# Queries and keys of the dilated groups stay in natural order, and TensorE reads every fourth column of them

## The chip, the cores and the metric

The kernel runs on one core of a Trainium2 chip. The metric is the time of one execution on the device in microseconds, the median of the runs shown. One more execution was taken by the profiler; the views below are of that one. Engines are named as in the profile: PE is TensorE's matmuls, PEld its loads of the stationary operand, DVE is VectorE, ACT is ScalarE, POOL is GpSimd and SP is SyncE.

## The reference, cut to what matters

Two layers over 512 positions of width 1024, in float32. Each layer is a half feed-forward step, a mixer, a second half feed-forward step and a gated embedding. The mixer of layer 0 (the even one) holds two attentions that share one projection: a windowed one, and a dilated one, which the change touches. The dilated one has 12 heads of 64, in three groups of four slots, and the outputs of the three groups are merged by their softmax denominators:

```python
B_PAIRS = ((128, 1), (512, 4), (2048, 16))        # window, dilation of the three groups
def dilated_attention(q, k, v):
    for gi, (window, dil) in enumerate(B_PAIRS):
        def to_res(t):        # positions sorted into residue classes modulo dil
            return t.reshape(bsz, sub, dil, B_SLOTS, dh).transpose(0, 2, 1, 3, 4).reshape(bsz * dil, sub, B_SLOTS, dh)
        o, lse = banded_attention(to_res(q), to_res(k), to_res(v), window // (2 * dil))
```

`q` and `k` have a rotary embedding before that: each half of a head's 64 features is multiplied by a cosine of the position and gets the other half times a sine added.

## The kernel before, in words

Activations lie with features on the 128 partitions and the 512 positions along the free dimension, 4 bytes each. Weights are split into a high and a low part, and each product of the projections is three matmuls of 128x128 by 128x512 (`mm3`, lines 171 to 173).

The even mixer (`ab`, line 621) is a list of attention steps (`a_steps`, `b_steps`) into which a second list, the projections and value projections (`fill`), is woven by weights written out by hand (`weave`, line 714): a projection is put in front of the step that needs it, or earlier where its share of the work has come. TensorE works through its part of this in program order, so while VectorE and ScalarE prepare a step's operands, TensorE runs a projection.

The dilated attention handles two slots at a time (`sp` is 0 or 1). For each slot pair, `proj_b` projects and rotates the queries and keys of group 0 (`stacked`) and of groups 1 and 2 (`proj`); the latter stay in plain float32. `rope` (line 578) is where a projection leaves PSUM: two VectorE instructions multiply it by the sine (L595, into `u`) and by the cosine (L596, into `o`), each reading the 512 columns of the PSUM bank in order, and four DMAs with an accumulating write (L599, issued from GpSimd's queue) add the 32-row pieces of `u` to the swapped pieces of `o`. `kind` gives the order in which the two instructions write: "n" natural, "b" (queries of group 0) by blocks of 128 and, within them, by residue modulo 4, and "r" (groups 1 and 2) by residue modulo 4 over all 512 positions, so that a write in kind "r" hops 128 elements from one column to the next. Twenty ropes run in the mixer: ten "n", two "b", eight "r".

In `b_steps`, `soft` makes the scores. Group 0 goes through `scores` (L612, L613). For groups 1 and 2 there is, for each residue r, one product of 64x128 by 64x128 for each group (L820), with 128 contiguous columns of `bq` as the stationary and of `bk` as the moving operand, since kind "r" has sorted them; the profile shows each such float32 product as two matmul records. A VectorE reduction with the mask follows (L824), the exponentials are ScalarE's (L830). `merge` combines the denominators of the groups with small copies between partitions (L840, L857) and scales all exponentials (L861); `pv_r` transposes the scaled tiles on TensorE (L870), copies them out (L872) and multiplies them with the values (L876); `pv_n` does the same for group 0 (`windows_pv`: L531, L147 and L148, L541 and L542), and L891 adds the two, reading both of its sources in hops. L906 is an addition of the same size without hops.

Of the kernel before, what the change touches and what calls it, by code (L numbers as in the profile page):

```python
# [15 lines left out]
P = 128  # L16
# [29 lines left out]
class Trunk:  # L46
# [530 lines left out]

    def rope(self, p, kind):


        nc = self.nc
        if self.cosr is None:
            self.cosr, self.sinr = self.act(), self.act()
            nc.vector.tensor_tensor(self.cosr, self.rot[0], self.R, op=ALU.mult)
            nc.vector.tensor_tensor(self.sinr, self.rot[1], self.R, op=ALU.mult)

        o, u = self.act(), self.tmp()
        if kind == "n":
            v = w = lambda x: x
        elif kind == "r":  # L590
            v, w = (lambda x: x.rearrange("p (r a) -> p a r", r=4)), (lambda x: x.rearrange("p (a r) -> p a r", r=4))
        else:
            v, w = (lambda x: x.rearrange("p (b r a) -> p b a r", b=NB, r=4)), (lambda x: x.rearrange("p (b a r) -> p b a r", b=NB, r=4))
        with self.tc.high_priority():
            nc.vector.tensor_tensor(v(u), w(p), w(self.sinr), op=ALU.mult)  # L595
            nc.vector.tensor_tensor(v(o), w(p), w(self.cosr), op=ALU.mult)  # L596
        for i in range(4):
            j = i ^ 1
            nc.gpsimd.dma_start(o[i * 32:(i + 1) * 32, :], u[j * 32:(j + 1) * 32, :], accum_op=ALU.add)  # L599
        return o  # L600
# [20 lines left out]
    def ab(self, k_next):  # L621
        nc, io = self.nc, self.io
        cos, sin = self.act(), self.act()
        nc.sync.dma_start(cos, io["cos"])
        nc.sync.dma_start(sin, io["sin"])
        self.rot, self.cosr = (cos, sin), None
        m_a, m_b0, m_br = self.act(), self.act(), self.act()
        nc.sync.dma_start(m_a[:, :384], io["mask_a"])
        nc.sync.dma_start(m_b0[:, :384], io["mask_b0"])
        nc.sync.dma_start(m_br[:, :256], io["mask_br"])  # L630
        sink = self.small("sink", [P, 12])
        nc.sync.dma_start(sink, io["sink"].partition_broadcast(P))
        self.turn, self.alone = 1, True
        mix = [None] * KC
        w = io["qk_ab"]

        nat = lambda x, b: x[:, b * P:(b + 1) * P]
        v = {}

        t = {}  # L640

        def proj(key, i, kind):
            return [(key, 1, lambda: t.__setitem__(key, self.rope(self.project(w[i]), kind)))]

        def stacked(key, i, kind, p=None):

            c = []

            def stack():
                if key[0][1] == "k":  # L650
                    low = self.lows()
                    t[key] = (self.stack_k(c[0], low), low)
                else:
                    t[key] = self.stack_q(c[0])

            return [(key + (0,), 1, lambda: c.append(self.rope(p or self.project(w[i]), kind))), (key, 0, stack)]

        def behind_next(*items):

            out, rest = [], []  # L660
            for first, *second in items:
                out += [first] + rest
                rest = second
            return out + rest

        def proj_a(gp):
            return [stacked(("ak", gp), 12 + 4 * gp, "n")] + [
                stacked(("aq", gp, j), 13 + 4 * gp + j, "n") for j in range(3)]

        def proj_b(sp):  # L670
            out = [stacked(("bk", sp, 0), 6 * sp + 1, "n"), stacked(("bq", sp, 0), 6 * sp, "b")]
            for g in (1, 2):
                out.append(proj(("bq", sp, g), 6 * sp + 2 * g, "r"))
                out.append(proj(("bk", sp, g), 6 * sp + 2 * g + 1, "r"))
            return out

        def proj_v(key, i):
            if i < 2:
                f = lambda: v.__setitem__(key, self.project_v(io["v_ab"][i], nat, self.rcol))
            else:  # L680
                f = lambda: v.__setitem__(key, self.residues(
                    self.project_v(io["v_ab"][i], nat, self.rcol, parts=False)))
            return [(key, 2.4, f)]


        p = [self.project(w[12 + i], self.sbank()) for i in range(2)]
        with self.tc.issue_after(self.last_mm.ins):
            self.R
        fill = behind_next(stacked(("ak", 0), 12, "n", p[0]), stacked(("aq", 0, 0), 13, "n", p[1]), proj_v("va", 0),
                           *proj_a(0)[2:], *proj_a(1), *proj_b(0), proj_v("vb", 1), proj_v(("vr", 0), 2),  # L690
                           *proj_b(1), proj_v(("vr", 1), 3))
        steps = (self.a_steps(0, t, v, m_a, sink, mix) + self.a_steps(1, t, v, m_a, sink, mix)
                 + self.b_steps(0, t, v, m_b0, m_br, mix) + self.b_steps(1, t, v, m_b0, m_br, mix))
        fill += [(("o", m), PART, lambda m=m: self.out_part(io["o_ab"], m, mix, range(6))) for m in range(OPEN)]
        for _ in range(6):
            fill.pop(0)[2]()
        kept = self.put_away()

        first = steps[0][2]

        def behind():
            with self.tc.issue_after(self.last_mm.ins):
                first()

        steps[0] = steps[0][0], steps[0][1], behind

        for i in BEGIN_B:
            steps[i - 2] = steps[i - 2][0] + steps[i][0], *steps[i - 2][1:]
        self.weave(steps, fill, after={("o", 0): BEGIN_B[0]})
        self.alone = False  # L710
        self.out_proj(io["o_ab"], mix, 6, k_next, kept)
# [85 lines left out]
    def b_steps(self, sp, t, v, m_b0, m_br, mix):  # L797
# [4 lines left out]
        nc = self.nc  # L802
        c = {}

        def soft(hf):

            if hf == 0:
                c["st"] = self.small("st_b", [P, 2, 2, 2, 4])
            st = c["st"][:, hf]
            ng = self.small("ng_b", [P, 2, 4])  # L810
            e0 = [self.scores(t["bq", sp, 0], t["bk", sp, 0], hf, b, (m_b0, st[:, 0, 0, b:b + 1])) for b in range(NB)]
            rows = slice(hf * HD, (hf + 1) * HD)
            er = []
            for r in range(0, 4, 2):
                s = self.sbank()
                e = self.act()
                for i in range(2):
                    rr = slice((r + i) * P, (r + i + 1) * P)
                    for g in (1, 2):
                        nc.tensor.matmul(s[:, (2 * i + g - 1) * P:(2 * i + g) * P], t["bq", sp, g][rows, rr],  # L820
                                         t["bk", sp, g][rows, rr], start=True, stop=True)
                for i in range(2):
                    x = slice(2 * i * P, 2 * (i + 1) * P)
                    nc.vector.tensor_tensor_reduce(e[:, x], s[:, x], m_br[:, :256], op0=ALU.add, op1=ALU.max,  # L824
                                                   scale=0.125, scalar=-3e38, accum_out=st[:, 0, 1, r + i:r + i + 1])
                    er.append(e[:, x])
            nc.vector.tensor_scalar_mul(ng, st[:, 0], -1.0)
            for g, es in ((0, e0), (1, er)):
                for i, e in enumerate(es):
                    nc.scalar.activation(e, e, AF.Exp, bias=ng[:, g, i:i + 1], accum_out=st[:, 1, g, i:i + 1])  # L830
            c["e0", hf], c["er", hf] = e0, er
# [51 lines left out]
        def pv_n(hf):  # L883
# [9 lines left out]
            if hf:  # L893
                mix[6 + sp] = self.split_chunk(c["raw"], nc.vector)

        qk = [(x, sp, g) for x in ("bq", "bk") for g in range(3)]
        return [(qk, 1.5, lambda: soft(0)), (qk, 1.5, lambda: soft(1)), ([], 2, merge),
                ([("vr", sp)], .7, pv_r), (["vb"], 1.2, lambda: pv_n(0)), ([], 1.2, lambda: pv_n(1))]

# [384 lines left out]
```

## Time and profile before

| what | value |
|---|---|
| median of 3 runs | 2052.24 us (2050.88 to 2056.14) |
| the profiled execution, its own time | 2054.03 us |
| its span in the profile | 2052.3 us |
| mean granted clock of TensorE | 0.995 |
| busy: PE, PEld, DVE, ACT, POOL | 99%, 88%, 68%, 49%, 11% of the span |
| the even mixer | about 369 to 663 us of the span |

[...]

### The profile page before, as it was taken

What the parts mean: (1) busy time and instruction counts of PE and PEld (TensorE: products, weight loads), DVE (VectorE), ACT (ScalarE), POOL (GpSimd) and SP (SyncE); (2) the same over time, 40 slices, a digit from 0 to 9 for tenths busy, and PEclk for the clock granted to TensorE, in tenths of its full rate; (3) what the DMA queues carried; (4) which work ended last, traced back from release to release, by engine and by line L of the source; (5) the groups of instructions that cost most, each with busy time, mean ns of one, the idle gap of its engine ahead of it and who ended that gap; (6) DMA issues with size and microseconds to landing.
All of it is one profiled execution on the core that took longest, in us unless ns stands there. A gap on an engine that the chain in (4) does not pass through costs nothing.

```text
span 2052.3 us, 32118 instructions
## 1 busy us (share of the span) xinstructions
PE 2025.7 (99%) x12398; PEld 1806.6 (88%) x12398; DVE 1389.3 (68%) x2389; ACT 1008.5 (49%) x1702; POOL 229.0 (11%) x230
## 2 busy tenths in 40 slices
PE   9999999999999999999999999999999999999998
PEld 6999988888778899988888999888888889998886
DVE  8888733598866888843468888434778688885344
ACT  6555522476544555532345555323666545554232
POOL 0001011332212000001110000011000100000111
PEclk9999999999999999999999999999999999999999
DMA  6666543453335466643344665544333446764331
GB/s 196 181 184 181 162 131 129 113 114 82 85 75 176 107 182 181 167 148 111 118 134 125 183 180 158 154 132 141 107 103 112 154 107 168 188 178 134 111 108 42
DMA packets 111515, 284.25 MB, mean 139 GB/s; under 512 B 21761, under 2 KB 29441, under 8 KB 111361
## 3 DMA queue, kind: packets, MB, share of 16 engines
q1 hardware_dynamic: 97584, 241.26, 36.4%
q0 software_dynamic: 13632, 40.90, 12.7%
q8 instruction: 97, 1.59, 0.3%
q14 instruction: 58, 0.47, 0.1%
q10 hardware_dynamic: 144, 0.04, 0.0%
HBM read 258.03 MB, written 13.07 MB: 132 GB/s over the span
## 4 chain that ended last, share of the span: by engine, by line
PE 89%; DVE 4%; ACT 2%; issue 2%; DMA 1%; POOL 1%; SPq 0%; DVEq 0%; ACTq 0%; POOLq 0%
PE mm L172 10%; PE mm L171 10%; PE mm L173 10%; PE mm L360 6%; PE mm L359 6%; PE mm L358 6%; PE sc L171 6%; PE sc L173 6%; PE sc L172 6%; PE sc L360 3%; PE sc L358 3%; PE sc L359 3%; PE ob L358 2%; PE ob L360 2%; PE ob L359 2%
## 5 line engine op out<-in xcount | busy, mean ns | idle before, releaser
L147 ACT ACTIVATE wh<-wr 128x1024 fp32r<-128x1024 f32 (+2 forms) x431 | 446.5, 1038 | 641.2 <-PE mm L172 180.6
L148 DVE TENSOR_TENSOR wl<-wr,wh 128x1024 fp32r<-128x1024 f32 (+2 forms) x431 | 518.1, 1204 | 336.3 <-ACT wh L147 334.0
L171 PE MATMUL mm<-act,wh 128*128 128x512 f32 (+1 forms) x1000 | 391.8, 392 | 0.7 <-ACT act L197 0.4
L172 PE MATMUL mm<-act,wh 128*128 128x512 f32 (+1 forms) x1000 | 391.1, 391 | 0.7 <-DVE act L198 0.6
L173 PE MATMUL mm<-act,wl 128*128 128x512 f32 (+1 forms) x1000 | 390.2, 390 | 0.0
L360 PE MATMUL mm<-act,wl 128*128 128x256 f32 x1088 | 307.9, 283 | 0.0
L359 PE MATMUL mm<-act,wh 128*128 128x256 f32 x1088 | 307.9, 283 | 0.0
L358 PE MATMUL mm<-act,wh 128*128 128x256 f32 x1088 | 307.9, 283 | 0.0
L173 PE MATMUL sc<-act,wl 128*128 128x512 f32 x610 | 237.3, 389 | 0.4 <-DVE wl L148 0.4
L171 PE MATMUL sc<-act,wh 128*128 128x512 f32 x610 | 237.3, 389 | 0.0
L172 PE MATMUL sc<-act,wh 128*128 128x512 f32 x610 | 237.1, 389 | 0.0
L172 PEld LDWEIGHTS mm<-act,wh 128*128 128x128 f32 x1000 | 188.4, 188 | 38.3 <-DVE act L198 2.2
L171 PEld LDWEIGHTS mm<-act,wh 128*128 128x128 f32 x1000 | 188.3, 188 | 37.3 <-ACT act L197 0.9
L173 PEld LDWEIGHTS mm<-act,wl 128*128 128x128 f32 x1000 | 188.3, 188 | 36.0
L359 PEld LDWEIGHTS mm<-act,wh 128*128 128x128 f32 x1088 | 208.9, 192 | 0.4
L360 PEld LDWEIGHTS mm<-act,wl 128*128 128x128 f32 x1088 | 208.9, 192 | 0.2
L358 PEld LDWEIGHTS mm<-act,wh 128*128 128x128 f32 x1088 | 208.9, 192 | 0.2
L212 POOL TENSOR_TENSOR ssq<-ssq,tmp 128x512 f32<-128x512 f32 x48 | 76.3, 1590 | 864.0 <-ACT tmp L205 670.3
L358 PE MATMUL sc<-act,wh 128*128 128x256 f32 x544 | 154.0, 283 | 0.0
L359 PE MATMUL sc<-act,wh 128*128 128x256 f32 x544 | 154.0, 283 | 0.0
L360 PE MATMUL sc<-act,wl 128*128 128x256 f32 x544 | 154.0, 283 | 0.0
L173 PEld LDWEIGHTS sc<-act,wl 128*128 128x128 f32 x610 | 114.5, 188 | 24.1 <-DVE wl L148 0.6
(177 smaller groups left out, 3427.5 us busy)
## 6 DMA issues: line engine op xcount, KB each, us to landing
wr<-in_gu_dram SPq DMA_DIRECT2D x176, 512.0 KB, 4.6
wr<-in_gu_dram POOLq DMA_DIRECT2D x68, 512.0 KB, 5.5
wr<-in_dn_dram SPq DMA_DIRECT2D x64, 512.0 KB, 3.6
rb<-in_gu_dram SPq DMA_DIRECT2D x68, 256.0 KB, 3.0
wr<-in_dn_dram SPq DMA_DIRECT2D x32, 384.0 KB, 3.5
kept<-act SPq DMA_DIRECT2D x40, 256.0 KB, 2.2
wr<-in_qk_ab_dram SPq DMA_DIRECT2D x20, 512.0 KB, 3.3
act<-kept SPq DMA_DIRECT2D x40, 256.0 KB, 4.3
```

The source lines that it names most:

```text
L147: self.put(self.nc.scalar.activation(hi, src, AF.Copy))
L148: self.put((lo_eng or self.nc.vector).tensor_tensor(lo, src, hi.bitcast(F32), op=ALU.subtract))
L171: mm(out, stat[0], mov[0], start=start, stop=False)
L172: mm(out, stat[0], mov[1], start=False, stop=False)
L173: return mm(out, stat[1], mov[0], start=False, stop=stop)
L212: eng.tensor_tensor(self.acc, self.acc, sq, op=ALU.add)
L358: mm(out, w[0][:, c], xs[k][0][:, x], start=start and k == 0, stop=False, skip_group_check=True)
L359: mm(out, w[0][:, c], xs[k][1][:, x], start=False, stop=False, skip_group_check=True)
L360: mm(out, w[1][:, c], xs[k][0][:, x], start=False, stop=stop and k == half - 1, skip_group_check=True)
```

## The change

`rope` loses its kind "r", the projections of groups 1 and 2 use kind "n" instead, so that their queries and keys stay in natural order, and L820 takes the columns of a residue with a step of four, in the stationary and in the moving operand. Values, masks and everything behind the scores stay as they are, since the scores come out in the same order as before.

```diff
@@ def rope(self, p, kind):
         if kind == "n":
             v = w = lambda x: x
-        elif kind == "r":
-            v, w = (lambda x: x.rearrange("p (r a) -> p a r", r=4)), (lambda x: x.rearrange("p (a r) -> p a r", r=4))
         else:
@@ def proj_b(sp):
             for g in (1, 2):
-                out.append(proj(("bq", sp, g), 6 * sp + 2 * g, "r"))
-                out.append(proj(("bk", sp, g), 6 * sp + 2 * g + 1, "r"))
+                out.append(proj(("bq", sp, g), 6 * sp + 2 * g, "n"))
+                out.append(proj(("bk", sp, g), 6 * sp + 2 * g + 1, "n"))
             return out
@@ def soft(hf):
                 for i in range(2):
-                    rr = slice((r + i) * P, (r + i + 1) * P)
                     for g in (1, 2):
-                        nc.tensor.matmul(s[:, (2 * i + g - 1) * P:(2 * i + g) * P], t["bq", sp, g][rows, rr],
-                                         t["bk", sp, g][rows, rr], start=True, stop=True)
+                        nc.tensor.matmul(s[:, (2 * i + g - 1) * P:(2 * i + g) * P], t["bq", sp, g][rows, r + i::4],
+                                         t["bk", sp, g][rows, r + i::4], start=True, stop=True)
```

## Rows read from the trace of the kernel before

**Rows 1.** Head of the page: busy time (share of span) xinstructions.

```profile
span 2052.3 us, 32118 instructions
PE 2025.7 (99%) x12398; PEld 1806.6 (88%) x12398; DVE 1389.3 (68%) x2389; ACT 1008.5 (49%) x1702; POOL 229.0 (11%) x230
```

**Rows 2.** The chain that ended last, shares of the span by engine.

```profile
PE 89%; DVE 4%; ACT 2%; issue 2%; DMA 1%; POOL 1%; SPq 0%; DVEq 0%; ACTq 0%; POOLq 0%
```

**Rows 3.** Stretches: length, busy us (xinstructions) of PE, PEld, DVE, ACT, POOL, clock, DMA.

```profile
440.00:487.00 47.00, 46.21 (x241) 37.02 (x240) 43.11 (x99) 31.07 (x72) 18.12 (x24) 1.00 0.53 105
487.00:512.00 25.00, 24.80 (x194) 23.96 (x193) 19.92 (x61) 18.09 (x49) 3.19 (x4) 1.00 0.30 76
...
545.00:553.50 8.50, 8.50 (x39) 6.95 (x37) 8.14 (x26) 5.92 (x12) 3.44 (x7) 1.00 0.54 127
553.50:557.60 4.10, 0.29 (x2) 0.00 (x0) 3.81 (x21) 0.00 (x0) 1.48 (x2) 0.78 0.89 181
557.60:562.60 5.00, 4.96 (x15) 4.00 (x16) 5.00 (x16) 0.00 (x0) 0.00 (x0) 0.50 0.01 1
562.60:576.00 13.40, 13.32 (x91) 10.39 (x91) 7.75 (x11) 5.86 (x11) 3.18 (x4) 1.00 0.42 99
576.00:580.00 4.00, 3.18 (x24) 2.60 (x21) 4.00 (x6) 1.83 (x3) 2.31 (x5) 1.00 0.22 23
...
603.00:607.40 4.40, 2.53 (x12) 1.75 (x11) 3.81 (x24) 1.11 (x3) 0.00 (x0) 1.00 0.17 54
```

**Rows 4.** Waits of TensorE, 440 to 630 us: total, times, longest.

```profile
PE tr L870 <- DVE act L861: 5.7, 2, 3.9
PE ob L542 <- DVE tmp L148: 0.7, 1, 0.7
PE sc L612 <- DVE st_b L613: 0.5, 1, 0.5
```

**Rows 5.** Timeline of DVE: start, duration, engine, line, operation.

```profile
528.50 0.69 DVE L595 TENSOR_TENSOR tmp<-mm,act 128x512 f32<-128x512 f32 x1 [0.96 <-PE mm L173]
529.11 0.68 DVE L596 TENSOR_TENSOR act<-mm,act 128x512 f32<-128x512 f32 x1
...
547.23 1.11 DVE L595 TENSOR_TENSOR tmp<-mm,act 128x512 f32<-128x512 f32 x1
548.16 1.39 DVE L465 TENSOR_TENSOR act<-act,act 64x512 fp32r<-64x512 f32 x2
...
550.17 1.09 DVE L596 TENSOR_TENSOR act<-mm,act 128x512 f32<-128x512 f32 x1
...
576.08 1.09 DVE L596 TENSOR_TENSOR act<-mm,act 128x512 f32<-128x512 f32 x1
577.01 1.08 DVE L595 TENSOR_TENSOR tmp<-mm,act 128x512 f32<-128x512 f32 x1
577.92 1.06 DVE L596 TENSOR_TENSOR act<-mm,act 128x512 f32<-128x512 f32 x1
578.83 0.41 DVE L148 TENSOR_TENSOR tmp<-tr,tmp 128x256 fp32r<-128x256 f32 x1
```

**Rows 6.** Timeline of PE, same columns; x16 are sixteen records merged.

```profile
532.57 2.05 PE L820 MATMUL sc<-act,act 64*128 64x128 f32 x16
534.54 0.50 PE L172 MATMUL mm<-act,wh 128*128 128x512 f32 x1
...
557.64 0.69 PE L870 MATMUL tr<-ident,act 128*128 128x128 f32 x2 [3.85 <-DVE act L861]
...
563.35 1.15 PE L876 MATMUL ob<-tmp,act 128*64 128x128 f32 x16
...
579.29 0.39 PE L542 MATMUL ob<-tmp,act 128*128 128x256 f32 x1 [0.75 <-DVE tmp L148]
```

**Rows 7.** Groups of instructions by form: busy us, mean ns of one.

```profile
L891 DVE TENSOR_TENSOR act<-tmp,tmp 64x512 f32<-64x512 f32 x4 | 4.9, 1235 | 0.1
L906 DVE TENSOR_TENSOR tmp<-ob,tmp 64x512 f32<-64x512 f32 x4 | 2.7, 683 | 5.0 <-ACT tmp L905 5.0
```

## The prediction

> **What bounds the kernel now.** I read the head of the profile first: the matmul row of TensorE is busy for 2025.7 of 2052.3 us, so all of its idle time is 26.6 us, and every other engine has slack [rows 1]. The chain of work that ended last says the same: 89% of it is TensorE, 4% VectorE [rows 2]. What VectorE saves therefore shows in the time only where TensorE stands and waits for VectorE, and what TensorE loses shows nearly everywhere. The table by stretches looks for such places in the even mixer, from 440 us, where the first rope of a dilated group is still to come, to the last merge at 607 us [rows 3]. [...] The waits name the releasers: the two merges (L870 after the scaling at L861) 5.7 us in two waits, the longest 3.9; L542 after the low part of a transposed tile at L148, 0.7; L612 after a score reduction, 0.5 [rows 4]. These are the only doors through which a faster VectorE can shorten the run.
>
> **Part 1: the rope's two VectorE writes.** The change lets eight of the twenty ropes (two slot pairs, groups 1 and 2, q and k) write in natural order. Each is two instructions, L595 and L596, so 16 instructions change their write from one that hops 128 elements between neighbours to a plain one. Both kinds are in the trace, with the same reads from PSUM and SBUF [rows 5]. A plain one (528.50) lasts 0.69 us and the next starts 0.61 us behind it. A hopping one (547.23, 550.17, 576.08, 577.01, 577.92) lasts 1.06 to 1.11 and the next instruction starts 0.91 to 0.93 behind it (547.23, 576.08, 577.01, 577.92). The start to start difference is what VectorE gains: 0.31 us each, 16 x 0.31 = 5.0 us of VectorE's time. That is the whole possible gain, and most of it lies under TensorE's work. Door by door:
>
> The merge of slot pair 0. VectorE is at work nearly without a pause on the way to the scaling that TensorE waits for (8.14 of the 8.5 us from 545 to 553.5, and on through the gap [rows 3]), and two hopping writes of one rope stand in its queue, at 547.23 and 550.17. With both plain, the small copies and the scaling behind them come 0.6 us sooner, and TensorE's wait of 3.85 us, which ends at 557.64 [rows 6], becomes about 3.2. Gain 0.6 us. Bounds: if the chain is held by ScalarE's exponentials rather than VectorE, 0; if the shorter gap leaves the clock up, the 5.0 us at 0.50 become 2.5, so 0.6 + 2.5 = 3.1 us.
>
> The wait of L542 at 579.29 for the L148 at 578.83. In front of that L148 stand three hopping writes in a row (576.08, 577.01, 577.92), of which the last two belong to one rope and delay it, with the first, by 0.9 us. TensorE waited 0.75 us there [rows 6]; this door closes. Gain 0.75 us, bounds 0 (something else just as late, for instance ScalarE's part of the same tile) and 0.82, all the idle time of that stretch.
>
> The fourth rope of slot pair 1 writes between 562.8 and 564.8, in a stretch in which TensorE is idle for 0.08 us in all [rows 3]: worth nothing. The eight writes of slot pair 0 stand between 460 and 487 us. TensorE's whole idle time there and up to 512 is 0.79 + 0.20 = 0.99 us, in pieces, and only part of it waits for VectorE (the 0.5 us of L612). I take 0.2 us, bounds 0 and 0.99.
>
> The second merge, at 607.36, has no rope in front of it any more (the last ends at 578.8), so its 1.87 us stay. The two ropes of group 0 kept in their own order and the ten plain ones are untouched. The accumulating DMAs at L599, four for each rope, move the same rows of 512 contiguous elements, in the same number, from the same queue, and no wait is added: a rope's copies may start a little sooner, no more. The sum of part 1 is -0.6 - 0.75 - 0.2 = -1.55 us.
>
> **Part 2: TensorE reads every fourth column.** L820 issues 32 products, seen as 64 matmul records of 64x128 with one load of 128 columns each. Both operands now step four elements (16 bytes) between columns, the stationary and the moving one. Sixteen of them run from 532.57 to 534.54, 0.123 us each. No row of the trace shows TensorE reading with such a step, so I bound it. Below by 0: a stepped read has no reason to be quicker than a plain one. How near the memory these streams run can be read from L876: the same 128 moving columns against only 64 loaded ones take 1.15 / 16 = 0.072 us [rows 6]. So the moving stream has at least 0.05 us to spare for each record, and the load has none: 64 columns more cost 0.05 us, 0.8 ns a column, and any slowing of the load shows in full. Above by what a hop costs VectorE: the hopping write 0.31 us / 512 = 0.61 ns an element; or the two-source hopping read of L891 against the plain L906, 1.235 - 0.683 = 0.55 us / 512 = 1.08 ns [rows 7]. On 64 x 128 = 8192 loaded columns that is 5.0 us or 8.8 us, all on TensorE, which is busy in these stretches. I take 0: both prices are those of another engine's ports with other instructions, and the rows nearest to it, L820 and L876 on TensorE itself [rows 6], say that its load takes 0.8 ns a column where its moving stream needs at most 0.072 us / 128 = 0.56 ns for one, so that the load is not at the pace that these ports can read. This is the weakest step, and both ends stay in the range.
>
> [...]
>
> **Sum.** -1.55 + 0 = -1.55 us. The profiled execution took 2054.03 us (span 2052.3 and 1.7 around it), so it would take 2052.5. It lies 1.8 us above the median of the runs shown, 2052.24; from that median the same sum gives 2050.7 us.
>
> **The rivals.**
> *TensorE pays for the step.* This is the one that ends on the other side. Place: the 64 loads of L820. Price 5.0 to 8.8 us, net of part 1 +3.5 to +7.3, that is 2055.7 to 2059.5 us. It decides the sign as soon as a record takes 1.55 / 64 = 0.024 us more than 0.123; it is told from no change (0.3%, 6.2 us, about what a measurement of this kernel can tell) when it takes 7.7 / 64 = 0.12 us more, twice today's pace. For it: the load has no slack, and VectorE's rows show that this memory makes hopping streams dearer by half or more. Against it: the ports are others, and the moving side has slack.
> *Nothing reaches the end.* VectorE's 5 us all lie under TensorE, or what is gained at 557 and 579 is lost at the next wait (the second merge waits for ScalarE's exponentials and the 16 copies at L857 whatever came earlier). Then 2052.2 us. For it: 99% busy. Against it: the two waits whose releasers stand right behind hopping writes.
> [...]
> *Another order.* The program orders instructions of several queues around the ropes (L595 and its L596 are often split by others, as at 547.23 and 550.17). If the shorter operations lead to another order, waits of the size seen in rows 4 may open or close: 2 to 7 us either way.
>
> **How the numbers follow.** Forecast 46%, nothing reaches the end 12%, the clock stays up 8%, TensorE pays 26% (half of it, 13%, above +6.2, since both reads of a record may pay, one after the other), another order 8% (of which 4% faster by more than 6.2, 2% slower by more). Faster by over 0.3% needs 6.2 us, more than all of part 1's bounds add up to (3.1 + 0.82 + 0.99 = 4.9), so it is left to another order and what was overlooked: 6%. Slower by over 0.3%: 13 + 2 + 1 for what was overlooked = 16%. Within: 78% (the two shares for what was overlooked come off the forecast). The forecast's own range is 2048.5 to 2052.5; the range that should hold 8 in 10 reaches down to all of part 1's gains, 2052.2 - 4.9 = 2047.3, and up to the dearer price short of its end, 2059.
>
> **What the changed profile would show.** L595 and L596: sixteen fewer at 1.06 to 1.1 us, leaving two hopping ropes; the VectorE total falls by some 5 us. The wait of L870 at the first merge near 3.2 us and no wait of L542 for L148 show the doors right; the same waits unchanged show rival two. The sixteen records of L820: 1.97 us from the first to the next matmul if the step is free; 3.2 us or more if it pays. The granted clock behind the first merge: 0.50 for some 5 us, or not at all. The forecast is wrong if L820 takes over 2.4 us for sixteen, or if a new wait of more than 1 us appears on TensorE.

## The result, and the profile after

The changed kernel takes 2063.47 us in the median of 6 runs (2058.91 to 2067.34), the kernel before 2054.76 us on the same chip (6 runs, 2050.88 to 2056.19). The ratio is 1.0046 with a 95% interval of 1.0036 to 1.0055, that is +9.4 us (7.4 to 11.3): slower, and above the range that was forecast. (The ratio is the one estimated from the single runs, here and below, and not exactly that of the two medians.) The profiled execution of the changed kernel took 2058.91 us, the quickest of its six: its mean granted clock (the profile gives TensorE's clock as a share of full speed) is 0.996, that of the slowest run 0.991, so the trace shows less of what the clock costs than the median does.

Each engine's instructions stand in the same order in both programs; sixteen of VectorE's have another access pattern, and so have TensorE's score products. So every difference between the traces is one of durations and of what follows from them. Lines have moved up by three or four: L592 and L593 are L595 and L596 of before, L609 is L612, L816 is L820, L857 is L861, L866 is L870.

The head of the page after, and the chain by engine, as in [rows 1, 2]:

```profile
span 2057.1 us, 32118 instructions
PE 2031.2 (99%) x12398; PEld 1813.6 (88%) x12398; DVE 1384.3 (67%) x2389; ACT 1007.3 (49%) x1702; POOL 228.9 (11%) x230
...
PE 90%; DVE 3%; ACT 2%; issue 2%; DMA 1%; POOL 1%; SPq 0%; DVEq 0%; ACTq 0%; POOLq 0%
```

VectorE's busy time fell by 5.0 us, just as forecast, TensorE's rose by 5.5. The timeline of VectorE after shows the writes that stood in front of the low part L148 in [rows 5]:

```profile
577.63 0.68 DVE L593 TENSOR_TENSOR act<-mm,act 128x512 f32<-128x512 f32 x1
578.23 0.68 DVE L592 TENSOR_TENSOR tmp<-mm,act 128x512 f32<-128x512 f32 x1
578.83 0.68 DVE L593 TENSOR_TENSOR act<-mm,act 128x512 f32<-128x512 f32 x1
579.42 0.41 DVE L148 TENSOR_TENSOR tmp<-tr,tmp 128x256 fp32r<-128x256 f32 x1
```

The writes last 0.68 us in place of 1.06 to 1.09, and the next starts 0.60 us behind. The waits of TensorE after, for [rows 4]:

```profile
PE tr L866 <- DVE act L857: 5.1, 2, 3.2
PE sc L609 <- DVE st_b L610: 0.5, 1, 0.5
PE sc L609 <- DVE st_a L610: 0.3, 1, 0.3
```

The wait at the first merge went from 3.9 to 3.2 us, and that of L542 for L148 is gone. So VectorE's part came as forecast at these two doors. What it was traded for stands in the timeline of TensorE after, for [rows 6]:

```profile
529.70 0.39 PE L173 MATMUL mm<-act,wl 128*128 128x512 f32 x1
529.93 0.40 PE L171 MATMUL mm<-act,wh 128*128 128x512 f32 x1
530.26 4.13 PE L816 MATMUL sc<-act,act 64*128 64x128 f32 x16
534.32 0.79 PE L172 MATMUL mm<-act,wh 128*128 128x512 f32 x1
534.91 0.63 PE L609 MATMUL sc<-act,act 128*128 128x256 f32 x2
535.34 0.63 PE L173 MATMUL mm<-act,wl 128*128 128x512 f32 x1
```

From the first of the sixteen records to the next matmul it is now 534.32 - 530.26 = 4.06 us, 0.254 us a record, where it was 1.97 us and 0.123. (Records overlap in the rows: the L173 at 529.70 lasts 0.39 us, and the next begins 0.23 us behind it, so pace is read from start to start. Both averages hold some 0.2 us for the two ends of a block; within it a record starts every 0.235 us, where it was 0.112, as the rows under e7 show.) And the matmuls behind the block last 0.63 us, where those ahead of it last 0.39. The table by stretches says why, and answers to [rows 3]:

```profile
512.00:545.00 33.00, 33.00 (x168) 28.69 (x167) 19.27 (x56) 16.93 (x44) 4.22 (x6) 0.95 0.27 73
...
556.70:560.10 3.40, 0.22 (x1) 0.00 (x0) 3.11 (x21) 0.00 (x0) 0.63 (x1) 1.00 0.86 201
560.10:564.80 4.70, 4.64 (x18) 3.57 (x18) 4.70 (x17) 0.30 (x1) 0.00 (x0) 0.64 0.01 1
...
578.00:582.00 4.00, 3.93 (x32) 3.64 (x31) 3.86 (x7) 2.21 (x4) 3.16 (x7) 1.00 0.40 40
...
533.90:537.50 3.60, 3.60 (x13) 2.99 (x12) 1.34 (x8) 1.37 (x5) 0.00 (x0) 0.54 0.39 134
```

From 512 to 545 us the profile shows no gap on TensorE, and yet the mean granted clock is 0.95: from 533.9 to 537.5, at the end of the first stepped block and behind it, the mean is 0.54, so that nearly all of this stretch is at 0.50 (all of 534.0 to 537.0 is). The gap in front of L866 ends before the clock falls now, but it falls behind it (0.64 from 560.1 to 564.8).

Both traces can be laid side by side at the same instructions, with the chain's rows. First the kernel before:

```profile
371.57 1.12 PE tr L238 x4
...
414.62 0.58 PE sc L612 x4
...
532.63 1.98 PE sc L820 x16
537.72 1.98 PE sc L820 x16
...
588.94 1.98 PE sc L820 x16
594.06 1.98 PE sc L820 x16
...
661.28 0.79 PE tr L219 x8
```

Then the changed one:

```profile
371.92 0.65 PE tr L238 x4
...
413.50 0.59 PE sc L609 x4
...
530.33 4.06 PE sc L816 x16
538.81 4.05 PE sc L816 x16
...
589.74 4.05 PE sc L816 x16
596.94 4.05 PE sc L816 x16
...
666.20 0.79 PE tr L219 x8
```

The changed kernel is 0.35 us behind at 371, 2.30 ahead at the first block, 1.09 behind at the second (2.08 for the block, 1.3 for the clock behind it), 0.80 behind at the third (its gains at the merge and at L542 lie between), 2.88 behind at the fourth and 4.92 behind at the end of the mixer, where it stays (span +4.8). Four blocks of +2.07 make +8.3 us. The gain ahead of the first block, 2.65 us, is not all the change's: the L238 at 371 already runs at the lower clock in the trace before (0.50 from 371.5 to 374.5; 1.12 us for four, against 0.65 at 1.00), and at 414 us, where no rope of the change has run yet, the changed kernel is 1.12 us ahead. So 1.47 us of the 2.65 are a clock that fell at the start of the mixer in one execution and not in the other, and 1.2 us are the change's. Term by term this trace gives 8.3 (blocks) + 1.3 (clock) - 1.2 - 2.3 (the gains ahead of the first and of the third block) - 1.1 (the start of the mixer) = +5.0 us, against 4.92.

### The profile page after: what moved, and what is told of

It reads as the page before. It is cut to its first block, busy times and chain, and to the rows that moved or that the text cites. A ratio compares the mean times of both kernels' runs of the same rounds, so it can differ in the third digit from the quotient of the medians.

```text
span 2057.1 us, 32118 instructions
## 1 busy us (share of the span) xinstructions
PE 2031.2 (99%) x12398; PEld 1813.6 (88%) x12398; DVE 1384.3 (67%) x2389; ACT 1007.3 (49%) x1702; POOL 228.9 (11%) x230
## 4 chain that ended last, share of the span: by engine, by line
PE 90%; DVE 3%; ACT 2%; issue 2%; DMA 1%; POOL 1%; SPq 0%; DVEq 0%; ACTq 0%; POOLq 0%
PE mm L172 10%; PE mm L171 10%; PE mm L173 10%; PE mm L360 6%; PE mm L359 6%; PE mm L358 6%; PE sc L171 6%; PE sc L173 6%; PE sc L172 6%; PE sc L360 3%; PE sc L359 3%; PE sc L358 3%; PE ob L358 2%; PE ob L360 2%; PE ob L359 2%
## 5 line engine op out<-in xcount | busy, mean ns | idle before, releaser
L148 DVE TENSOR_TENSOR wl<-wr,wh 128x1024 fp32r<-128x1024 f32 (+2 forms) x431 | 518.0, 1204 | 335.1 <-ACT wh L147 331.2
L172 PE MATMUL mm<-act,wh 128*128 128x512 f32 (+1 forms) x1000 | 391.3, 391 | 0.6 <-DVE act L198 0.6
L173 PE MATMUL mm<-act,wl 128*128 128x512 f32 (+1 forms) x1000 | 390.6, 391 | 0.0
L173 PE MATMUL sc<-act,wl 128*128 128x512 f32 x610 | 237.3, 389 | 0.4 <-DVE wl L148 0.4
L172 PE MATMUL sc<-act,wh 128*128 128x512 f32 x610 | 237.1, 389 | 0.0
L172 PEld LDWEIGHTS mm<-act,wh 128*128 128x128 f32 x1000 | 188.5, 189 | 38.3 <-DVE act L198 2.0
L173 PEld LDWEIGHTS mm<-act,wl 128*128 128x128 f32 x1000 | 188.3, 188 | 36.0 <-issue 0.2
L173 PEld LDWEIGHTS sc<-act,wl 128*128 128x128 f32 x610 | 114.5, 188 | 24.0 <-DVE wl L148 0.6
```

What stands on the lines that cost most here:

```text
L148: self.put((lo_eng or self.nc.vector).tensor_tensor(lo, src, hi.bitcast(F32), op=ALU.subtract))
L172: mm(out, stat[0], mov[1], start=False, stop=False)
L173: return mm(out, stat[1], mov[0], start=False, stop=stop)
```

## The experiments

All are edits of the kernel before, which leave each engine's order of instructions as it was, but for e6.

**e1: only the queries, the loaded operand, are stepped.**

```diff
-                out.append(proj(("bq", sp, g), 6 * sp + 2 * g, "r"))
+                out.append(proj(("bq", sp, g), 6 * sp + 2 * g, "n"))
-                        nc.tensor.matmul(s[...], t["bq", sp, g][rows, rr],
+                        nc.tensor.matmul(s[...], t["bq", sp, g][rows, r + i::4],
```

> Only the queries change: the query ropes of groups 1 and 2 write in natural order and the score matmuls load every fourth column as the stationary operand; keys stay sorted, so the moving operand is contiguous. Theory A (the load pays for the step): the 64 score records take about 0.25 us each as in the changed kernel (sixteen in some 4.05 us), the time is 6 to 9 us above the kernel before. Rival B (the moving stream pays): records stay at 0.12 to 0.13 us and the time is within 1 us of before, or a little below. Rival C (each operand pays half): records of about 0.19 us, +4 us.

Ratio 1.0053 (1.0039 to 1.0066), median 2062.66 against 2053.06 us. The first block in its timeline, from start to next start 4.03 us, 0.252 a record:

```profile
530.50 4.10 PE L820 MATMUL sc<-act,act 64*128 64x128 f32 x16
534.53 0.79 PE L172 MATMUL mm<-act,wh 128*128 128x512 f32 x1
```

By itself this fits theory A, that the load pays. The time lies above the +6 to +9 us expected; the expectation left out the clock, which is 0.79 in the mean from 526 to 545 us here.

**e2: only the keys, the moving operand, are stepped.**

```diff
-                out.append(proj(("bk", sp, g), 6 * sp + 2 * g + 1, "r"))
+                out.append(proj(("bk", sp, g), 6 * sp + 2 * g + 1, "n"))
-                                         t["bk", sp, g][rows, rr], start=True, stop=True)
+                                         t["bk", sp, g][rows, r + i::4], start=True, stop=True)
```

> Only the keys change: the key ropes of groups 1 and 2 write in natural order and the score matmuls stream every fourth column as the moving operand; queries stay sorted, so the loaded operand is contiguous. Theory A (the load pays for the step): records stay at 0.12 us, the time is within 1 us of before, or up to 1.5 us below. Rival B (the moving stream pays): records of 0.25 us, +6 to +9 us. Rival C (each pays half): records of about 0.19 us, +4 us.

Ratio 1.0049 (1.0037 to 1.0062), median 2063.03. Theory A falls as well as B and C: the moving stream alone costs nearly the whole price, 3.79 us for the block, 0.237 a record. The two don't add up (both stepped: 0.254), so the load of one record and the stream of another go on side by side, and either one alone sets nearly the same pace.

```profile
530.83 3.87 PE L820 MATMUL sc<-act,act 64*128 64x128 f32 x16
534.62 0.80 PE L172 MATMUL mm<-act,wh 128*128 128x512 f32 x1
```

**e3: sorted half way, in pairs.** The rope writes two neighbours, then hops; TensorE reads every second column. The 16-byte line of the expectations here, under e7 and under e9 is four neighbouring columns of 4 bytes; that a read's price goes by it was the author's supposition, which e7 and e9 test.

```diff
-            v, w = (lambda x: x.rearrange("p (r a) -> p a r", r=4)), (lambda x: x.rearrange("p (a r) -> p a r", r=4))
+            v, w = (lambda x: x.rearrange("p (h a l) -> p a h l", h=2, l=2)), (lambda x: x.rearrange("p (a h l) -> p a h l", h=2, l=2))
-                    rr = slice((r + i) * P, (r + i + 1) * P)
+                    rr = slice((r + i) // 2 * 256 + (r + i) % 2, (r + i) // 2 * 256 + 256, 2)
```

> Queries and keys are sorted half way: the rope writes in the order (upper bit of the residue, position, lower bit), so that VectorE writes runs of two neighbours and TensorE reads every second column. If the price hangs on a step of a whole 16-byte line for each column, records stay at 0.12 to 0.13 us, the 16 rope writes take 0.68 us as plain ones, and the time is 1 to 2 us below before. Rival (any step pays): records of 0.19 to 0.25 us and the time +3 to +8 us. Rival on VectorE's side: the writes stay at 1.0 us and more, and the time is that of before.

Ratio 0.9990 (0.9981 to 0.9999), median 2051.23 against 2053.06. Its block takes 2.08 us, 0.130 a record, and no clock is lost there:

```profile
529.99 2.15 PE L820 MATMUL sc<-act,act 64*128 64x128 f32 x16
532.07 0.50 PE L172 MATMUL mm<-act,wh 128*128 128x512 f32 x1
```

VectorE's writes of pairs are as quick as plain ones (0.69 and 0.68 us in [rows 5]): the median L595 of this kernel lasts 0.685 us, 1.068 before, and only the two of the ropes of kind "b" are left at 1.1.

**e4: VectorE's half of the change alone.** The ropes write in natural order, TensorE reads neighbours as before.

```diff
-                out.append(proj(("bq", sp, g), 6 * sp + 2 * g, "r"))
-                out.append(proj(("bk", sp, g), 6 * sp + 2 * g + 1, "r"))
+                out.append(proj(("bq", sp, g), 6 * sp + 2 * g, "n"))
+                out.append(proj(("bk", sp, g), 6 * sp + 2 * g + 1, "n"))
```

> VectorE's half of the change alone: the ropes of groups 1 and 2 write in natural order and the score matmuls still read 128 neighbouring columns, so the scores of groups 1 and 2 are those of blocks of positions, not of residue classes. Forecast of the prediction for this part: 1.55 us below before (bounds 0 and 4.9), the sixteen rope writes at 0.68 us, records at 0.12 us. Rival: nothing reaches the end, the time of before within 0.5 us.

Ratio 0.9991 (0.9983 to 1.0000), median 2051.57: -1.8 us (-3.5 to 0), near the -1.55 of the sum, with an interval that reaches no change. The chain of its trace, to be laid beside that of the trace before above:

```profile
414.59 0.58 PE sc L612 x4
...
531.40 1.98 PE sc L820 x16
...
590.52 1.98 PE sc L820 x16
...
659.26 0.79 PE tr L219 x8
```

The two are level at 414 us. At the first score block e4 is 1.23 us ahead: the eight writes (four ropes) of slot pair 0 gave some 1.2 us, not 0.2. At the fourth block it is 3.54 us ahead, and at the end of the mixer 2.02: what is lost between lies behind the second merge, where the clock fell in this execution and stayed at 1.00 in the one before:

```profile
604.40:607.70 3.30, 3.30 (x10) 2.62 (x10) 3.30 (x13) 0.00 (x0) 0.00 (x0) 0.50 0.11 35
```

**e5: TensorE's half alone.** The ropes sort as before, the score products read with the step.

```diff
-                        nc.tensor.matmul(s[...], t["bq", sp, g][rows, rr], t["bk", sp, g][rows, rr], ...)
+                        nc.tensor.matmul(s[...], t["bq", sp, g][rows, r + i::4], t["bk", sp, g][rows, r + i::4], ...)
```

> TensorE's half of the change alone: the ropes still sort the columns (their writes hop as before), and the score matmuls read every fourth column of the sorted operands, in both, so that the scores are those of other columns. Theory 1 (the step costs 0.13 us a record and, besides, the granted clock falls behind the stepped blocks): 64 x 0.13 = 8.3 us plus 1 to 4 us, that is +9 to +12, and stretches at 0.50 right behind or inside the four score blocks. Theory 2 (the records' pace alone): +8.3 us within 0.5, the clock falling only behind the first merge.

Ratio 1.0056 (1.0043 to 1.0069), +11.5 us, median 2065.01 against 2053.87. In its profiled execution four blocks of 4.05 us, and, of the stretches at the lower clock, two with TensorE busy throughout, behind the first block and behind the third:

```profile
536.50:539.50 3.00, 3.00 (x10) 2.43 (x9) 1.29 (x7) 1.01 (x3) 0.00 (x0) 0.51 0.42 167
...
596.00:602.00 6.00, 6.00 (x30) 5.78 (x29) 3.10 (x15) 2.08 (x7) 0.00 (x0) 0.72 0.24 85
```

**e6: the same length without a step.** Each score product is issued twice.

```diff
+                        for _ in range(2):
-                        nc.tensor.matmul(s[...], t["bq", sp, g][rows, rr], t["bk", sp, g][rows, rr], ...)
+                            nc.tensor.matmul(s[...], t["bq", sp, g][rows, rr], t["bk", sp, g][rows, rr], ...)
```

> The kernel before with each score product of groups 1 and 2 issued twice into the same place: 128 records that read neighbouring columns, so that TensorE is at these products about as long as with the stepped reads, but at its usual pace (0.124 us a record, a block of 32 in 3.95 us). If the clock falls in the changed kernel because a stepped record keeps TensorE's array waiting for its operands, it stays at 1.00 around the four blocks here, and the time is +7.9 us within 1, 1 to 4 us less than the kernel with the stepped reads alone. If longer score blocks as such bring the clock down (what is issued behind them comes late), stretches at 0.50 appear here too, and the time is the same as there.

Ratio 1.0033 (1.0020 to 1.0046), median 2060.28: +6.8 us, where four blocks of 3.77 us in place of 1.98 make +7.2. Around the blocks the clock stays up, with TensorE just as busy:

```profile
526.00:536.00 10.00, 10.00 (x64) 8.68 (x63) 5.95 (x22) 1.06 (x1) 4.22 (x6) 1.00 0.60 161
536.00:540.00 4.00, 4.00 (x29) 3.43 (x29) 1.61 (x10) 3.87 (x15) 0.00 (x0) 1.00 0.02 4
...
590.00:602.00 12.00, 12.00 (x98) 11.45 (x97) 6.78 (x31) 4.32 (x17) 0.00 (x0) 1.00 0.13 44
```

The block is shorter than the 3.95 us expected. e5 is 4.7 us above e6 in the medians of the same chip, five executions of each. The blocks explain 8.3 - 7.2 = 1.1 of it; the other 3.6 us are no matter of the blocks' length. They fit the clock: it is 0.9944 in the mean of e5's five executions and 0.9962 in that of e6's, and 0.0018 of 2062 us are 3.7 us at full speed. Not all of it need come from the steps. In the two profiled executions the stretches behind e5's first and third blocks are worth 3.0 x 0.49 + 6.0 x 0.28 = 3.2 us at most, an estimate; e5 has two more that e6 hasn't (0.76 from 370 to 377 us, ahead of anything that the edit touches, and 0.76 from 616 to 623).

**e7: every third column.**

```diff
-                    rr = slice((r + i) * P, (r + i + 1) * P)
+                    rr = slice(r + i, r + i + 3 * P, 3)
```

> The kernel before with the score matmuls of groups 1 and 2 reading every third column of the sorted operands (scores of other columns). If the price is one access for each new 16-byte line, three of four columns are in a new line and sixteen records take about 0.75 of the way from 2.0 to 4.05 us, some 3.0 to 3.6 us. If any step that leaves no two columns in each line pays in full: 4.05 us. If only a step of a whole line pays: 2.0 to 2.1 us.

One run, 2061.48 us. The block takes 3.06 us, 0.191 a record:

```profile
533.00 3.13 PE L820 MATMUL sc<-act,act 64*128 64x128 f32 x16
536.06 0.80 PE L172 MATMUL mm<-act,wh 128*128 128x512 f32 x1
```

The ends of a block are in this average. Pieces of the chain from within the first block show the pace without them, in this order: the kernel before, step 2 (e3), step 3 (this run), step 4 of the moving operand alone (e2), step 4 of both (the changed kernel):

```profile
532.94 1.12 PE sc L820 x10
...
530.49 1.41 PE sc L820 x12
...
533.50 2.11 PE sc L820 x12
...
531.29 2.72 PE sc L820 x12
...
530.86 2.35 PE sc L816 x10
```

That is 0.112 us a record without a step, 0.118 with a step of 2, 0.176 with 3, 0.227 and 0.235 with 4 (and 0.233 in e1). If four columns of 4 bytes share a line of 16 bytes, 128 columns touch 64 lines with a step of 2, 96 with 3 and 128 with 4: 1.84, 1.83 and 1.77 to 1.84 ns a line. The pace goes by lines; 128 neighbours touch 32 lines and go at 0.112, so something else than lines limits them.

**e8: e3 once more.**

> The half sorted kernel once more (VectorE writes runs of two neighbours, TensorE reads every second column): 1 to 3 us below before, sixteen records in 2.08 us; the question is only whether the interval of the ratio lies below 1 again.

Ratio 0.9986 (0.9977 to 0.9995), median 2051.06 against 2053.87. The interval lies below 1 again. This version beats both kernels, by 2 to 3 us against the kernel before.

**e9: neighbours in pairs, with a hop of eight between them**, in the moving operand alone.

```diff
-                    rr = slice((r + i) * P, (r + i + 1) * P)
+                    rr = lambda x: x.rearrange("p (a e) -> p a e", e=8)[rows, :, r + i:r + i + 2]
-                        nc.tensor.matmul(s[:, (2 * i + g - 1) * P:(2 * i + g) * P], t["bq", sp, g][rows, rr],
-                                         t["bk", sp, g][rows, rr], start=True, stop=True)
+                        nc.tensor.matmul(s[:, (2 * i + g - 1) * P:(2 * i + g) * P], t["bq", sp, g][rows, (r + i) * P:(r + i + 1) * P],
+                                         rr(t["bk", sp, g]), start=True, stop=True)
```

> The kernel before with only the moving operand changed: it takes two neighbouring columns, hops to the next group of eight and takes two again, beginning at column 0, 1, 2 or 3 of the group for the four residues (scores of other keys). If the price is one access for each new line of 16 bytes: the records that begin at 0, 1 and 2 find both columns of a pair in one line, 64 lines of 1.9 ns, and stay at 0.12 us; those that begin at 3 have the pair across two lines and go to 0.24 us; so of the sixteen records of a block twelve are quick and four, the last, are slow: 12 x 0.124 + 4 x 0.24 = 2.4 us. If every hop pays, whatever the line: 64 hops, all sixteen alike, 2.0 us if a hop hides under the load, or up to 3 us.

One run, 2056.64 against 2052.54 us, too few to read the time. The block takes 2.49 us, 2.4 were expected by lines. The chain, cut at a point within the block, shows the first twelve records, and with the next row where the block ends:

```profile
534.53 1.58 PE sc L820 x12
...
537.02 0.43 PE mm L172
```

Twelve records in 1.58 us, 0.132 each, and the last four, whose pairs lie across two lines, in 537.02 - 536.11 = 0.91 us, 0.228 each; in both figures one end of the block is included. A hop to every second line costs next to nothing; a second line for each pair costs about as much as in e2 (0.237). That the pairs from columns 0, 1 and 2 are quick and those from column 3 slow is what lines of 16 bytes give; by lines of 8 bytes those from column 1 would be slow too, by lines of 32 bytes none.

## Why the prediction was wrong, point by point

**The step that failed** is part 2's "I take 0". The term was 64 x 0.13 = +8.3 us. It lay inside the bounds that the prediction had worked out, 0 to 8.8, near the dearer one. The mistake was to set aside the only prices that the trace had because they were another engine's. Counted whole, VectorE's hopping write goes at 0.93 us / 512 = 1.8 ns an element [rows 5], and TensorE's hopping reads go at 1.8 ns a column (0.227 / 128 moving, 0.233 / 128 loaded). A plain element takes VectorE 1.2 ns and a plain column takes TensorE 0.112 / 128 = 0.9 ns, so the difference is dearer on TensorE, some 1.0 ns, than the 0.61 of VectorE's write; the 1.08 of L891's hopping read came close. Whether the two engines share the 1.8 ns for one reason, no run tests.

**"The moving stream has at least 0.05 us to spare."** It does, and that doesn't help it: from at most 0.56 ns a column it goes to 1.8, and its 0.227 us pass the 0.112 of a plain record by far (e2). A slack has to be compared with the whole of the price. Nor did the load's 0.8 ns a column leave room for a step: stepped, it goes to 1.8 (e1).

**The 16-byte line.** No row of the trace before shows TensorE's price for a line, and the sum gave it none. The runs show one, for both of TensorE's reads: a step of four fp32 elements puts each column in a new line (0.227 us a record moving, e2, and 0.233 loaded, e1), and two columns in each line are nearly enough (step 2, e3: 0.130 us a record, where 0.124 is a contiguous one, the ends of the block included). The price is some 1.8 ns a line (e2, e3, e7).

**The clock** was in no case of the prediction in this place: a loss of it around the score blocks stood at nothing, without a reason. The profile shows no gap on TensorE around the stepped blocks, and the clock fell all the same, in the profiled execution of every kernel with steps of 3 or 4 (the changed one, e1, e2, e5, e7), each time at the end of the first block or right behind it (the lowest mean of a stretch of 2 us there is 0.50 in the changed kernel and e1, 0.57 in e2, 0.51 in e5 and e7); it stayed at 1.00 around that block in the other six (the kernel before, e3, e4, e6, e8 and e9). e6 against e5 sets it at some 3.6 us, with the doubt said there; the trace of the changed kernel, its quickest execution, has 1.3 us of it. With it the sum for the change is +8.3 (records) + 3.6 (clock, as in e5) - 1.8 (VectorE, as in e4) = +10.1 us; measured +9.4 (7.4 to 11.3). What the chip looks at when it lowers the clock, the runs don't show; that it goes with stepped records and not with the length of the block, they do.

**Part 1 came near in sum, but not term by term, and that is partly luck.** (Its idle times, 0.79, 0.20, 0.82 and 1.87 us, are the length less TensorE's busy time in [rows 3].) VectorE gained 5.0 us; alone it brought -1.8 us (e4) against -1.55 forecast. The wait at the merge became 3.2 us, as forecast, and the wait of L542 went. But in the trace of e4 the gains up to the fourth block are 3.5 us and not 1.55: 1.2 at slot pair 0 against 0.2, and 2.3 at the merge and at L542 against 1.35, in part since a shorter stretch at 0.50 came with the shorter gap (some 3.4 us in e4 and 6.8 before, worked out from the means of stretches of 2 us). 1.5 us of it were lost again where the clock fell behind the second merge, which the prediction took to stay as it was. The 1.2 us lie even above the bound of 0.99. That bound took TensorE's idle time for all that can be gained, and a matmul's duration, 0.39 us where the next one can start after 0.23, hides part of a late start: in the trace before, the L612 at 465.58 starts 0.47 us behind the L172 at 465.11, of which 0.08 counts as idle.

**That the clock stays up** behind the first merge, which had 8%, came in part: in the changed kernel it fell later, and for a shorter stretch (0.50 from 561.1 to 564.5, where it was 555.8 to 562.6). The lead that this gave beside the shorter gap is some 0.65 us of the 2.5 that the bounds of part 1 had for it: the first L876 behind the merge stands at 563.35 before [rows 6] and its like at 565.22 after, 1.87 us behind, where L870 was 2.52 behind (557.64 and 560.16).

**The rival that TensorE pays** had the place right and the point of decision too: 0.12 us more a record was named as what can be told from no change, and 0.13 came. Its dearer half was held possible because both reads might pay one after the other; they pay side by side, and either alone brings the price (e1, e2). The range ended at 2059 us, short of the dearer price, and no case had a term for the clock here.

## What to carry to other kernels

Moving a permutation from a VectorE write to a TensorE read moves its price to the engine that bounds the kernel: count the 16-byte lines that each operand touches, loaded and moving, at some 1.8 ns a line (64 to 128 lines a record here), and compare that with the pace of a plain record (0.112 us here). A half permutation that leaves two fp32 neighbours in each line for the writer, and a step of two for the reader, costs next to nothing on both engines (e3, e8: 0.118 us a record, 0.685 us a write). Behind slow matmuls look at the granted clock too, even where TensorE shows no gap.

## What the runs showed of the hardware that was not expected

TensorE's fp32 reads from SBUF, the memory that holds the operands, go at some 1.8 ns for each 16-byte line touched, loaded (0.233 us for 128 lines) or moving (0.227), with steps of 2 to 4 (0.118 us for 64 lines, 0.176 for 96); 128 neighbours, 32 lines, take 0.112. The load of one record goes on beside the stream of another (both stepped 0.235, and not the sum of the two). The granted clock can fall to 0.50 at the end of a block of stepped records, or right behind it, with no gap on TensorE in the profile (mean 0.54 from 533.9 to 537.5 in the changed kernel). The stepped blocks themselves take nearly the same whether or not the clock is lower in part of them (e5: 4.06 us at a mean of 0.92, 4.05 at 1.00; e1: 4.03 at 0.83, 3.92 at 1.00). VectorE writes runs of two neighbouring fp32 elements at the pace of a plain write (e3: 0.685 us for 128x512 in the median, plain 0.68, hopping 1.068).
